# Three edits to the order of the first 450 microseconds of a transformer layer: gate columns stored as rows, later squares, earlier context products

## The chip, the cores and the metric

The kernel runs on one core of a Trainium2 chip. The metric is the device time of one execution in microseconds, the median of the runs. Engines are called as in the profile: PE (TensorE), DVE (VectorE), ACT (ScalarE), POOL (GpSimd), SP (SyncE, which here only issues transfers).

## What is computed

One layer over 1024 latent tokens and 256 context tokens of width 1024, in float32. Cut to what matters here:

```python
mod_lat = silu(c) @ w_ada + b_ada            # 6 x 1024 columns: sh1, sc1, gt1, sh2, sc2, gt2
mod_ctx = silu(c_ctx) @ w_ada + b_ada
h_lat = rmsnorm(x, g) * (1 + sc1) + sh1      # 1024 tokens
h_ctx = rmsnorm(ctx, g) * (1 + csc1) + csh1  # 256 tokens
rq, rk, rv, rg, nq, nk, nv, gates = split(h_lat @ w_in)
_, crk, crv, _, _, cnk, cnv, _ = split(h_ctx @ w_in)
...                                          # retention, neighbourhood attention over latent + context keys
x1 = x + gt1 * rmsnorm(merged @ w_o, g_post)
out = x1 + gt2 * rmsnorm(mlp(modulate(x1)), g_post_ffn)
```

The gates gt1 and gt2 (times the norm weights) are wanted late, as rows that multiply every token.

## The kernel before, in words

The kernel is written in program order, and a planner, which simulates the engines when the program is built, lays down the order of the instructions of each engine; each engine, and each transfer queue, then runs its own list in order. Where several instructions are ready in the simulation, the one that is earlier in the program goes first. `behind(ins)` forces the instructions of a block behind `ins` on its engine's list. Tiles come from pools of few buffers; a tile waits until the last reader of the buffer's former tile is done, and where one pool is closed and another opened on the same place, the new pool's tiles wait for the old pool's readers, transfers included.

Products are made in three passes of split float32 (`mm3`, lines 200 to 202): high x high, high x low and low x high, where `split` (lines 166, 167) casts the high part on ACT and subtracts the low part on DVE or POOL. Products of 512 (or 256) columns and eight blocks of the inner dimension are 24 instructions of PE. Their results lie in five PSUM banks taken in turn (`acc`), and ACT or DVE copies them out.

*Start.* The eight token tiles of x are loaded; `normed` (line 292) takes the squares' sums of four tiles on ACT (line 296), the reciprocal root on DVE (lines 214 to 225) and scales the tiles (line 299). `ada_first(p)` (line 323) makes the columns of shift and scale for a quarter of the width, with sixteen small products per weight block (line 332), and writes them to s1 and b1 (lines 338 to 341). `modulated` (line 311) turns a block of four tiles with PE (line 315), and writes the modulated block of hT (or of hc for the context): the high part by ACT (line 316), the full value hh by DVE (line 318), the low part by DVE or POOL (line 319). Line 345 normalises the first four tiles, line 349 the other four, and the loop from line 350 runs over the four quarters of the width.

*First projections.* `first` and `second` are the two weight chunks of the neighbourhood attention's keys, in two buffers of high and low parts. `fm_lat` makes their latent products (copied out at line 385, stored to k_na at line 392), `fm_ctx` their context products (copied to stc at line 398, stored to ck_na at line 399). The order in lines 434 to 437 is latent of first, latent of second, context of first, context of second. The weights of the values (`values`, line 488) are the next to be cast into these buffers (winhi by ACT at line 166, winlo by DVE at line 167). In between in the program stands the decay block (lines 440 to 465): z is loaded by SP, DVE makes zt (lines 443 to 454) with one exponential by ACT (line 445).

*Gate columns.* The rest of the modulation (`ada_rest`, line 405) is made in eight pieces, one beside each projection; the last one (n == 11) reads all of them back as columns (`columns`, line 272), multiplies the two gates by the norm weights (line 431), and POOL stores the columns [128, 8] to the rows `grow` in memory (line 432). They are read again at lines 955 and 1197. Then the pool `pb` is closed, and the neighbourhood stage opens its pool there; its keys kk are cast by ACT at line 623 and DVE at line 624, and enter PE's scores at line 648, among gate products (line 704) that fill PE.

Of the kernel before, what the change touches and what calls it, by code (L numbers as in the profile page):

```python
# [11 lines left out]
F32 = mybir.dt.float32  # L12
F32R = mybir.dt.float32r
AF = mybir.ActivationFunctionType
# [76 lines left out]
def block_kernel(ctx: ExitStack, tc: tile.TileContext, x, c, ctx_in, c_ctx, w_ada, b_ada, n_pre_mix, n_post_mix,  # L91
                 n_pre_ffn, n_post_ffn, w_in, decay_logit, w_ret_out, rpb, w_na_out, w_o, w_ff1, w_ff2, tab, out):
    nc = tc.nc
    v, a, g, pe, sy = nc.vector, nc.scalar, nc.gpsimd, nc.tensor, nc.sync
# [21 lines left out]
    def behind(ins):  # L116
        return nullcontext() if ins is None else tc.issue_after(ins.ins)
# [17 lines left out]
    def psum(tag):  # L135
        return ps.tile([128, 512], F32, name=tag, tag=tag, bufs=banks[tag])
# [5 lines left out]
    ident = const.tile([128, 128], F32, name="ident")  # L142
# [7 lines left out]
    def scratch(name, n, shape):  # L150
        return [dram.tile(shape, F32, name=f"{name}{k}") for k in range(n)]
# [10 lines left out]
    grow = scratch("grow", 2, [1, D])  # L162
# [79 lines left out]
    s1 = const.tile([128, 8, 2], F32, name="s1")  # L242
    b1 = const.tile([128, 8, 2], F32, name="b1")
# [17 lines left out]
    with ExitStack() as st:  # L261
        hT = [big.tile([128, 2, 8, 512], F32R, name="hT", tag=f"big{k}") for k in range(2)]
# [3 lines left out]
        def load_in(c0, **kw):  # L266
            return wp.load(w_in[0, :, c0:c0 + 256], 8, 256, **kw)
# [24 lines left out]
        def normed(tiles):  # L292
            n = len(tiles)
            ss = pa.tile([128, n], F32, name="ss", tag=f"ss{n}", bufs=2)
            for t, xt in enumerate(tiles):
                a.activation(hc[:, 1, 4:8, :].rearrange("p k n -> p (k n)"), xt[:], AF.Square, accum_out=ss[:, t:t + 1])
            r = rstd_of(pa, ss[:], n, f"x{n}")
            for t, xt in enumerate(tiles):
                v.tensor_scalar(xt[:], xt[:], r[:, t:t + 1], None, ALU.mult)

        xs, cxs, loads = [], [], []
# [9 lines left out]
        def modulated(xs, f, hi, lo, m, lo_eng):  # L311
            w = len(xs) * 128
            pt = psum("pt")
            for t, xt in enumerate(xs):
                pe.transpose(pt[:, t * 128:(t + 1) * 128], xt[:, f * 128:(f + 1) * 128], ident[:])
            a.activation(hi, pt[:, :w], AF.Identity, bias=b1[:, f, m:m + 1], scale=s1[:, f, m:m + 1])
            hh = pa.tile([128, 512], F32, name="hh", tag="hh", bufs=2)
            v.tensor_scalar(hh[:, :w], pt[:, :w], s1[:, f, m:m + 1], b1[:, f, m:m + 1], ALU.mult, ALU.add)
            lo_eng.tensor_tensor(lo, hh[:, :w], hi.bitcast(F32), op=ALU.subtract)

        pcol = psum("po")[:, 0:32].rearrange("p (b m) -> p b m", m=2)

# [23 lines left out]
        ada_first(0)  # L346
        first = load_in(2560, lo_eng=g, parts=4)
        loaded(x, 4, 8, xs)
        normed(xs[4:])
        for p in range(4):  # L350
            if p < 3:
                loads.append(ada_first(p + 1))
            if p == 1:
                second = load_in(2560 + 256, lo_eng=g)
            if p == 2:
                loaded(ctx_in, 0, 2, cxs, loads[2])
                normed(cxs)
            for half in range(2):
                for f in (2 * p, 2 * p + 1):
                    modulated(xs[half * 4:half * 4 + 4], f, hT[half][:, 0, f, :], hT[half][:, 1, f, :], 0, (v, g)[half])  # L360
            for f in {3: range(8)}.get(p, ()):
                modulated(cxs, f, hc[:, 0, f, :], hc[:, 1, f, :], 1, v)

# [13 lines left out]
        def fm_lat(w, ch, dst, p_, scale=1.0, silu=False, blocks=False):  # L377
            for f in range(2):
                stg = row()
                for half in range(2):  # L380
                    p = feature_major(w, lambda t, k: t[:, k, f * 128:(f + 1) * 128], half)
                    so = stg[:, half * 512:(half + 1) * 512]
                    if blocks:
                        so = stg[:].rearrange("p (b r c) -> p r b c", r=16, b=8)[:, half * 8:(half + 1) * 8]
                        a.activation(so, p[:].rearrange("p (r b c) -> p r b c", r=8, b=8), AF.Copy, scale=scale)
                    elif silu:
                        sgm = prb.tile([128, 512], F32, name="sgm", tag="kw", bufs=2)
                        a.activation(sgm[:], p[:], AF.Sigmoid)
                        v.tensor_tensor(so, p[:], sgm[:], op=ALU.mult)
                    else:  # L390
                        a.activation(so, p[:], AF.Copy, scale=scale)
                sy.dma_start(dst[ch * 2 + f][:], stg[:])

        def fm_ctx(w, r0, p_):
            for f in range(2):
                p = feature_major(w, lambda t, k: t[:, k, f * 128:(f + 1) * 128], 0, True)
                stc = p_.tile([128, NCTX], F32, name="stc", tag="stc", bufs=2)
                a.copy(stc[:], p[:])
                sy.dma_start(ck_na[r0 + f * 128:r0 + (f + 1) * 128, :], stc[:])
# [3 lines left out]
        pb = pool(st, "pb", 1)  # L403

        def ada_rest(n):
            ev = pb.tile([128, 512], F32, name="ev", tag="ev", bufs=1)
            for kb in range(2):
                w = wp.raw(4, 512)
                sy.dma_start(w[:], w_ada[0, kb * 512:(kb + 1) * 512, n * 512:(n + 1) * 512].rearrange("(k p) n -> p k n", p=128))
                for k in range(4):  # L410
                    s_ = cs[:, kb * 4 + k, 0:1]
                    if kb + k == 0:
                        v.tensor_scalar(ev[:], w[:, k, :], s_, None, ALU.mult)
                    else:
                        v.scalar_tensor_tensor(ev[:], w[:, k, :], s_, ev[:], ALU.mult, ALU.add)  # L415
            es = prb.tile([128, 2, 512], F32R, name="es", tag="kw", bufs=2)
            split(es[:, 0], es[:, 1], ev[:], lo_eng=g)
            pc = psum("po")[0:1, :]
            pe.matmul(pc, oner[:], es[:, 0], start=True, stop=False)
            pe.matmul(pc, oner[:], es[:, 1], start=False, stop=True)  # L420
            er = pb.tile([128, 512], F32, name="er", tag="ev", bufs=1)[0:1]
            a.copy(er, pc)
            sy.dma_start(arow[0:1, (n - 4) * 512:(n - 3) * 512], er)
            if n == 11:
                acol = pb.tile([128, 32], F32, name="acol")
                columns(pb, (arow[0],), acol[:])
                v.tensor_tensor(acol[:], acol[:], vt[:, 32:64], op=ALU.add)
                v.tensor_copy(b2[:], acol[:, 8:16])
                v.scalar_tensor_tensor(s2[:], acol[:, 16:24], 1.0, vt[:, 72:80], ALU.add, ALU.mult)
                for k, o in ((0, 0), (1, 24)):  # L430
                    v.tensor_tensor(acol[:, o:o + 8], acol[:, o:o + 8], vt[:, 80 + 8 * k:88 + 8 * k], op=ALU.mult)
                    g.dma_start(grow[k][0].rearrange("(k p) -> p k", p=128), acol[:, o:o + 8])

        fm_lat(first, 0, k_na, pb, blocks=True)
        fm_lat(second, 1, k_na, pb, blocks=True)
        fm_ctx(first, 0, pb)
        fm_ctx(second, 256, pb)


# [140 lines left out]
    with ExitStack() as sm:  # L580
# [6 lines left out]
        with ExitStack() as sn:  # L587
# [6 lines left out]
            for hp in range(4):  # L594
# [34 lines left out]
                for cb in range(8):  # L629
# [9 lines left out]
                    for e, (h, tbs, qs, ks) in enumerate(heads):  # L639
# [5 lines left out]
                        o = 0  # L645
# [32 lines left out]
                    for t in range(nb + 2):  # L678
                        for e in range(2):
# [6 lines left out]
                            last = pe.matmul(po[e * 64:(e + 1) * 64, o_:o_ + 128], l, r, start=(t == 0), stop=(t == nb + 1))  # L686
# [8 lines left out]
            for f, halves in [(f, (0, 1)) for f in range(NGB)] + [(f, (h,)) for h in range(2) for f in range(NGB, 16)]:  # L695
                w = wg.load(w_in[0, :, 3584 + f * 128:3584 + (f + 1) * 128], 8, 128, lo_eng=g)
                for half in halves:
                    hs = slice(half * 512, (half + 1) * 512)
                    stg = pn.tile([128, 512], F32, name="stg", tag="stg", bufs=3)
                    p = psum("mm")  # L700
# [147 lines left out]
        last = ret_finish(pna, *outs[3], lambda ob, hs: split(yr_[0][:, 3, hs], yr_[1][:, 3, hs], ob[:, hs]))  # L848


        for f in range(8):
            w = wn.load(w_na_out[0, :, f * 128:(f + 1) * 128], 4, 128, lo_eng=g)
            for half in range(2):
                hs = slice(half * 512, (half + 1) * 512)
                p = psum("mm")
# [12 lines left out]
    with sy_:  # L868
        pg = pool(sy_, "pg", 1)
        for f in range(8):  # L870
            w = wp.load(w_ret_out[0, :, f * 128:(f + 1) * 128], 4, 128, lo_eng=g)
            for half in range(2):
# [8 lines left out]
                p = acc()  # L881
                mm3(p[:], 4, lambda s_, k: w[s_][:, k, :], lambda s_, k: yr_[s_][:, k, hs])
                m = pg.tile([128, 512], F32, name="m", tag="m", bufs=2)
# [56 lines left out]
    with ExitStack() as s:  # L940
# [57 lines left out]
        xs = [php.tile([128, 2, D], F32, name="xn", tag="hp", bufs=2) for _ in range(2)]  # L998
# [21 lines left out]
        xs = [php.tile([128, 2, D], F32, name="xn", tag="hp", bufs=2) for _ in range(2)]  # L1020
# [53 lines left out]
        for j in range(EARLY):  # L1074
# [5 lines left out]
            with behind(turns[0] if j == EARLY - 1 else None):  # L1080
                p = product(acc(), ga, i + 1, b_1[:, 1])
# [4 lines left out]
        with behind(chain[-1]):  # L1086
            sums(raws[0])
            q3, last = third_sum(1)
# [101 lines left out]
    with ExitStack() as s:  # L1190
# [48 lines left out]
        for c4 in range(3):  # L1239
            w, new = home, None  # L1240
            for i, m in enumerate((m1, m2, m6, m3, m5, m7, m4)):
# [14 lines left out]
                for t in range(4):  # L1256
                    p = psum(next(turn8))
# [21 lines left out]
        for blkn in range(6, 8):  # L1279
# [15 lines left out]
            for t in range(8):  # L1295
# [8 lines left out]
                for cc in range(2):  # L1304
                    hs = slice(cc * 512, (cc + 1) * 512)
                    p = psum(next(turn8))
# [45 lines left out]
```

## Time and profile before

| | |
|---|---|
| runs | 1702.09, 1702.6, 1705.19 us; median 1702.6 |
| the profiled execution's own time | 1697.8 us |
| its span, first to last instruction | 1695.9 us |
| busy: PE, DVE, ACT, POOL | 96%, 58%, 38%, 20% of the span |
| mean granted clock of PE | 0.984 of full speed |

The span is what lies between the first and the last instruction of the trace; all times of instructions count from its start. The granted clock is the share of full speed that PE was given; 1.00 is 2.4 GHz and 0.50 is 1.2 GHz.

### The profile page before, as it was taken

To read this page: it belongs to the slowest core of one execution; us is meant where nothing else is said; L and a number is where in the kernel's file an instruction comes from. 1 tells how busy PE (TensorE), PEld (TensorE's weight loads), DVE (VectorE), ACT (ScalarE), POOL (GpSimd) and SP (SyncE) were. 2 spreads that over 40 slices of the span, in tenths; PEclk is the share of its full clock that TensorE was granted. 3 is DMA by queue.
4 is the path that set the end of the run, shared out by engine and by line. 5 is a ranking of instruction groups with operands and counts; after the bars stand their busy time and mean duration, and the time that the engine had idled before them with its cause. 6 is when DMAs were issued, how large, how long until landed. Compare 5 with 4: busy or idle time off the path is not lost. (4 is left out here: it accounts for less than half of the span.)

```text
span 1695.9 us, 21997 instructions
## 1 busy us (share of the span) xinstructions
PE 1622.1 (96%) x8547; PEld 1321.3 (78%) x8547; DVE 982.2 (58%) x1724; ACT 651.6 (38%) x912; POOL 338.9 (20%) x321
## 2 busy tenths in 40 slices
PE   5989999999999999989999998889999999999997
PEld 3889889988777777767776786668888878888885
DVE  5550244244345554565648657867776474778838
ACT  4321211112455555555346356334433365333311
POOL 1330022041322313357437001000010000000012
PEclk8999999999999999999999999999999999999998
DMA  9472644446523331276467424543354364423504
GB/s 326 163 172 71 185 137 150 145 131 190 148 72 121 98 101 62 87 207 179 137 229 250 163 84 142 176 166 112 138 179 168 132 253 149 173 101 111 183 30 149
DMA packets 156391, 252.95 MB, mean 149 GB/s; under 512 B 9776, under 2 KB 98872, under 8 KB 152576
## 3 DMA queue, kind: packets, MB, share of 16 engines
q1 hardware_dynamic: 145472, 213.05, 39.4%
q0 software_dynamic: 10816, 38.50, 6.4%
q8 instruction: 67, 1.10, 0.3%
q14 instruction: 36, 0.29, 0.1%
HBM read 184.18 MB, written 68.90 MB: 149 GB/s over the span
## 5 line engine op out<-in xcount | busy, mean ns | idle before, releaser
L166 ACT CAST wfhi<-wfraw 128x2048 fp32r<-128x2048 f32 (+2 forms) x47 | 62.0, 1357 | 175.7 <-PE sloc L201 36.9
L200 PE MATMUL mm<-hT,wghi 128*128 128x512 f32 x256 | 103.4, 404 | 0.0
L201 PE MATMUL mm<-hT,wghi 128*128 128x512 f32 x256 | 101.3, 396 | 0.0
L202 PE MATMUL mm<-hT,wglo 128*128 128x512 f32 x256 | 101.0, 395 | 0.0
L166 ACT CAST ops<-hr 128x2048 fp32r<-128x2048 f32 x20 | 38.2, 1909 | 113.2 <-PE mm L201 42.7
L167 DVE TENSOR_TENSOR wflo<-wfraw,wfhi 128x2048 fp32r<-128x2048 f32 (+2 forms) x47 | 74.2, 1605 | 5.8 <-ACT wfhi L166 5.8
L167 DVE TENSOR_TENSOR winlo<-winraw,winhi 128x2048 fp32r<-128x2048 f32 (+1 forms) x16 | 30.8, 1948 | 76.4 <-ACT winhi L166 76.4
L167 POOL TENSOR_TENSOR wglo<-wgraw,wghi 128x1024 fp32r<-128x1024 f32 x20 | 48.2, 2408 | 134.6 <-ACT wghi L166 134.5
L1312 POOL TENSOR_TENSOR m<-m,g 128x512 f32<-128x512 f32 x12 | 15.3, 1294 | 292.6 <-ACT jk L1311 292.6
L167 DVE TENSOR_TENSOR ops<-hr,ops 128x2048 fp32r<-128x2048 f32 x20 | 45.8, 2290 | 32.0 <-ACT ops L166 32.0
L166 ACT CAST winhi<-winraw 128x2048 fp32r<-128x2048 f32 (+2 forms) x21 | 27.4, 1335 | 95.5 <-PE sctx L201 48.8
L200 PEld LDWEIGHTS mm<-hT,wghi 128*128 128x128 f32 x256 | 48.4, 189 | 10.0 <-issue 2.2
L202 PEld LDWEIGHTS mm<-hT,wglo 128*128 128x128 f32 x256 | 48.5, 190 | 9.1 <-issue 0.3
L201 PEld LDWEIGHTS mm<-hT,wghi 128*128 128x128 f32 x256 | 48.4, 189 | 7.7 <-issue 0.2
L202 PE MATMUL sloc<-hT,winlo 128*128 128x512 f32 x136 | 53.3, 392 | 0.0
L200 PE MATMUL sloc<-hT,winhi 128*128 128x512 f32 x136 | 53.2, 392 | 0.0
L201 PE MATMUL sloc<-hT,winhi 128*128 128x512 f32 x136 | 53.1, 390 | 0.0
L201 PE MATMUL mm<-hT,winhi 128*128 128x512 f32 x120 | 47.4, 395 | 0.0
L415 DVE SCALAR_TENSOR_TENSOR ev<-winraw,cs,ev 128x512 f32<-128x512 f32 x56 | 44.6, 797 | 3.9 <-DMA winraw<-in_w_ada_dram 2.2
L202 PE MATMUL mm<-hT,winlo 128*128 128x512 f32 x120 | 46.8, 390 | 0.0
L607 POOL TENSOR_TENSOR tb<-tt,mask 128x128 f32<-128x128 f32 x56 | 29.4, 553 | 86.4 <-DVE mc L655 47.0
L200 PE MATMUL mm<-hT,winhi 128*128 128x512 f32 x120 | 46.4, 393 | 0.0
(1205 smaller groups left out, 5119.7 us busy)
## 6 DMA issues: line engine op xcount, KB each, us to landing
winraw<-in_w_ada_dram SPq DMA_DIRECT2D x24, 1024.0 KB
wfraw<-in_w_ff_dram SPq DMA_DIRECT2D x20, 1024.0 KB
winraw<-in_w_in_dram SPq DMA_DIRECT2D x14, 1024.0 KB
hs_d<-hs POOLq DMA_DIRECT2D x12, 1024.0 KB, 5.1
hr<-hs_d SPq DMA_DIRECT2D x12, 1024.0 KB
wgraw<-in_w_in_dram SPq DMA_DIRECT2D x20, 512.0 KB
gates<-stg POOLq DMA_DIRECT2D x32, 256.0 KB, 3.8
gg<-gates SPq DMA_DIRECT2D x32, 256.0 KB
```

The lines of the kernel that those rows point to most:

```text
L166: first = (hi_eng or a.copy)(hi_out, src)
L167: (lo_eng or v).tensor_tensor(lo_out, src, hi_out.bitcast(F32), op=ALU.subtract)
L200: pe.matmul(ps, lh, rh, start=(k == 0), stop=False)
L201: pe.matmul(ps, lh, rl, start=False, stop=False)
L202: pe.matmul(ps, ll, rh, start=False, stop=(k == ks - 1))
L415: v.scalar_tensor_tensor(ev[:], w[:, k, :], s_, ev[:], ALU.mult, ALU.add)
L607: g.tensor_tensor(tb[:, b * 128:(b + 1) * 128].rearrange("p (r c) -> p r c", c=8), tv[:, b0 + b], mask[:, c0 + b * 128:c0 + (b + 1) * 128] ...
L1312: (v if t >= 6 else g).tensor_tensor(y[cc], y[cc], g2[:, hs], op=ALU.mult)
```

## The change

There are three edits. `modulated` returns its ACT instruction, and the squares of the second four tiles are traced after the first half's two modulated blocks of the first quarter, with `behind`, in place of before the loop. The two finished gate columns, with the rest of their tile, are turned by one PE transpose into a PSUM bank, copied by DVE to a tile of rows and stored by POOL, eight rows of 128 floats for each gate, in place of the store of columns. And `fm_ctx(first)` is traced before `fm_lat(second)`.

```diff
-            a.activation(hi, pt[:, :w], AF.Identity, bias=b1[:, f, m:m + 1], scale=s1[:, f, m:m + 1])
+            first = a.activation(hi, pt[:, :w], AF.Identity, bias=b1[:, f, m:m + 1], scale=s1[:, f, m:m + 1])
...
             lo_eng.tensor_tensor(lo, hh[:, :w], hi.bitcast(F32), op=ALU.subtract)
+            return first
...
         loaded(x, 4, 8, xs)
-        normed(xs[4:])
         for p in range(4):
...
             for half in range(2):
                 for f in (2 * p, 2 * p + 1):
-                    modulated(xs[half * 4:half * 4 + 4], f, hT[half][:, 0, f, :], hT[half][:, 1, f, :], 0, (v, g)[half])
+                    last = modulated(xs[half * 4:half * 4 + 4], f, hT[half][:, 0, f, :], hT[half][:, 1, f, :], 0, (v, g)[half])
+                if p + half == 0:
+                    with behind(last):
+                        normed(xs[4:])
...
                 for k, o in ((0, 0), (1, 24)):
                     v.tensor_tensor(acol[:, o:o + 8], acol[:, o:o + 8], vt[:, 80 + 8 * k:88 + 8 * k], op=ALU.mult)
-                    g.dma_start(grow[k][0].rearrange("(k p) -> p k", p=128), acol[:, o:o + 8])
+
+                pt0 = psum("pt")
+                pe.transpose(pt0[:32, :128], acol[:], ident[:])
+                rows = pb.tile([32, 128], F32, name="rows", tag="rows32", bufs=1)
+                v.tensor_copy(rows[:], pt0[:32, :128])
+                for k, o in ((0, 0), (1, 24)):
+                    g.dma_start(grow[k][0].rearrange("(k p) -> k p", p=128), rows[o:o + 8, :])
 
         fm_lat(first, 0, k_na, pb, blocks=True)
+        fm_ctx(first, 0, pb)
         fm_lat(second, 1, k_na, pb, blocks=True)
-        fm_ctx(first, 0, pb)
         fm_ctx(second, 256, pb)
```

## Rows read from the trace of the kernel before

**Rows 1.** page of the profile, part 1: busy time of each engine.
```profile
PE 1622.1 (96%) x8547; PEld 1321.3 (78%) x8547; DVE 982.2 (58%) x1724; ACT 651.6 (38%) x912; POOL 338.9 (20%) x321
```

**Rows 2.** waits of PE, whole span: what it waited for: us in total, times, longest.
```profile
PE sctx L200 <- ACT hT L316: 4.3, 1, 4.3
PE sloc L648 <- DVE kk L624: 2.4, 1, 2.4
PE sloc L200 <- ACT winhi L166: 2.2, 1, 2.2
```

**Rows 3.** timeline of ACT: start us, us, line, operation, out<-in, count [idle before <-releaser].
```profile
19.77 2.18 ACT L166 CAST winhi<-winraw 128x512 fp32r<-128x512 f32 x4 [7.76 <-DMA winraw<-in_w_in_dram]
21.86 1.05 ACT L296 ACTIVATE hc<-xt 128x1024 fp32r<-128x1024 f32 x1
24.09 1.43 ACT L316 ACTIVATE hT<-pt,b,s 128x512 fp32r<-128x512 f32 x2
26.59 1.06 ACT L296 ACTIVATE hc<-xt 128x1024 fp32r<-128x1024 f32 x1
```

**Rows 4.** timeline of DVE, 20 to 33 us.
```profile
20.80 1.03 DVE L341 TENSOR_TENSOR s<-s,vt 128x2 f32<-128x2 f32 x2
30.15 2.74 DVE L299 TENSOR_SCALAR xt<-xt,r 128x1024 f32<-128x1024 f32 x4
```

**Rows 5.** timeline of PE, 29 to 35 us.
```profile
29.50 1.94 PE L332 MATMUL sloc<-winraw,cs 128*32 128x256 f32 x16
33.82 1.07 PE L332 MATMUL sloc<-winraw,cs 128*32 128x256 f32 x16
```

**Rows 6.** timeline of ACT, 92 to 106 us.
```profile
92.42 0.56 ACT L316 ACTIVATE hc<-pt,b,s 128x256 fp32r<-128x256 f32 x1 [0.56 <-PE pt L315]
102.95 0.21 ACT L445 ACTIVATE zt<-zt 128x16 f32<-128x16 f32 x1 [8.66 <-DVE zt L444]
103.33 1.90 ACT L166 CAST winhi<-winraw 128x2048 fp32r<-128x2048 f32 x1
```

**Rows 7.** timeline of SP's DMA queue, 88 to 96 us.
```profile
91.89 0.32 SPq L392 DMA_DIRECT2D k_na<-row  x1
92.31 2.25 SPq L441 DMA_DIRECT2D z<-in_ret_decay_logit_dram  x1
```

**Rows 8.** timeline of DVE, 93 to 109 us.
```profile
93.60 0.42 DVE L319 TENSOR_TENSOR hc<-hh,hc 128x256 fp32r<-128x256 f32 x1
102.53 0.18 DVE L443 TENSOR_SCALAR zt<-z 128x16 f32<-128x16 f32 x1 [8.51 <-DMA z<-in_ret_decay_logit_dram]
106.42 2.29 DVE L167 TENSOR_TENSOR winlo<-winraw,winhi 128x2048 fp32r<-128x2048 f32 x1
```

**Rows 9.** timeline of PE, at 108.77 us.
```profile
108.77 0.58 PE L201 MATMUL sloc<-winlo,hc 128*128 128x256 f32 x1 [2.06 <-DVE winlo L167]
```

**Rows 10.** busy by stretch: length; PE, PEld, DVE, ACT, POOL (instructions); granted clock, DMA share, GB/s.
```profile
27.06:29.50 2.44, 2.44 (x6) 1.50 (x6) 2.01 (x10) 0.68 (x2) 0.00 (x0) 0.50 1.09 349
108.77:113.70 4.93, 4.93 (x23) 4.93 (x24) 4.46 (x30) 0.58 (x2) 0.00 (x0) 0.50 0.83 254
448.24:451.40 3.16, 3.16 (x10) 2.68 (x11) 1.76 (x3) 2.21 (x4) 1.29 (x1) 0.50 0.44 123
```

**Rows 11.** timeline of DVE, 434 to 437 us.
```profile
434.59 0.19 DVE L283 COPY acol<-pt 128x32 f32<-128x32 f32 x1 [3.56 <-PE pt L282]
436.11 0.24 DVE L431 TENSOR_TENSOR acol<-acol,vt 128x8 f32<-128x8 f32 x2
```

**Rows 12.** timeline of POOL, then of ACT, 436 to 449 us.
```profile
436.78 1.80 POOL L432 DMA_DIRECT2D grow<-acol  x2
446.84 2.18 ACT L623 CAST kk<-kf 128x512 fp32r<-128x512 f32 x4 [10.88 <-DMA grow<-acol]
```

**Rows 13.** DMA issues: line's transfer, queue, count, KB each, median us from issue to landing.
```profile
grow<-acol POOLq DMA_DIRECT2D x2, 4.0 KB, 9.1
zp<-in_na_rpb_dram POOLq DMA_DIRECT2D x1, 14.5 KB, 2.1
```

## The prediction, made before the changed kernel was run

> **What bounds the kernel now.** I read the page's busy times first: PE is busy for 1622.1 of 1695.9 us [rows 1], so the kernel can get faster only where PE stands still or runs at the low clock, and every us of either that goes away is a us of the end, unless a new wait takes it. So the next view is what PE waited for, over the whole span [rows 2]; the reader is to see there three waits that touch lines of the change: 4.3 us for the first modulated block hT, 2.2 us for the weights winhi of the values, 2.4 us for kk, the first keys of the neighbourhood stage. The timelines around these three places say what held them, and the busy times by stretch say at which of its two clock levels PE came back: after each of them the granted clock was 0.50 (1.2 GHz) [rows 10].
>
> **First place, 20 to 33 us.** ACT is free of its weight casts at 21.95, the scale s1 is ready at 21.83 (20.80 + 1.03), but ACT then does two squares of the second half and turns to the first hT at 24.09 [rows 3, 4]. The change queues all four squares behind the two hT. ACT's work from 21.9 to 27.7 is the same in either order, so the squares still end at about 27.7 and DVE's scaling of the second half at 30.15 stays where it is. The first hT comes 24.09 - 21.95 = 2.1 us earlier, and with it PE's first product and DVE's remainder blocks behind it. The bounds are 0 and 2.1 us of gain. What PE can do with the time is little: six products, then the second block's sixteen column products (29.50), then transposes that need the scaled second half, then the next sixteen (33.82) [rows 5]. If the last ones move ahead of the transposes, as their weights come from a transfer and not from the squares, 1.07 us is won (their duration at full clock). I take 1.1. No DMA and no SP instruction moves with it. The cover of the second half's normalisation is ACT and DVE time in which PE has those products to do; gone, each us of delay of DVE's scaling at 30.15 is a us of PE. The added wait puts the squares behind the second hT on ACT; queued behind them is only the next hT, and DVE's square-root chain waits for them.
>
> **Second place, 92 to 114 us.** The four context products (24 products each) are the last PE work ahead of the values' weights. The weights of `first` sit in one of two buffers, and the values' first winhi takes that buffer, so it must wait until `fm_ctx(first)` has read it. Before, that is the third of four steps; with the change it is the second, with part of the second chunk's latent products and `fm_ctx(second)` still to come. The context blocks themselves are ready only at 94.02 (last remainder, 93.60 + 0.42) [rows 8], so the buffer can be free from about 94.5. But the buffer is not all that held the cast: ACT had nothing to do from 92.98 to 102.95, where it stood at the exponential of zt (L445), which waits for DVE, which waits for the transfer of z, issued at 92.31 and there at 102.53 [rows 6 to 8]. The cast follows at 103.33, its remainder winlo at 106.42, and PE's first product with winlo starts at 108.77 after another 2.06 us of idle [rows 6, 8, 9], and then runs 4.93 us at the low clock [rows 10].
> So the terms are: nothing, if cast and remainder stay behind the exponential; at the most both idle times, 2.2 + 2.06 (0.38 between them is small), and half of the low-clock stretch, 4.93 x 0.5 = 2.5, together 6.8; and below nothing, if the context copies (stc) are put behind the exponential on ACT: they hold PSUM banks until 103, and `fm_ctx(second)` cannot start; what it then does after 103 fills the stall that was there, so I price that at -0.5. Which of them it is depends on the order that the planner gives ACT and DVE. I expect the cast ahead of the exponential: it is ready at 94.5, while the transfer of z is only issued at 92.31 [rows 7]. DVE's first zt step stays ahead of winlo, and waits for z as now. Then winlo starts after z and three short steps, at 102.53 + 0.6 = 103.1 in place of 106.42 [rows 8]: 3.3 us. I take that and no gain of clock. Moved with the step are two stores of the context keys (SP), which come some us earlier, and the fourth store of k_na (91.89), which comes later, past z.
> That z is late is read in the rows: the 512 KB store of k_na went onto the same queue 0.4 us ahead of it, and z took 10.2 us [rows 7, 8]. The Trainium skill (DMA: Bandwidth & Descriptors, section "Queues, rings and completion order") says that each DMA engine takes turns between queue rows, packet by packet, and consumes one row's ring in order. By that rule z, with no store ahead of it in its own ring, would come earlier and the sum would take the third rival's value; no run here shows it.
>
> **Third place, 436 to 452 us.** The two gate columns are finished at 436.35 (436.11 + 0.24) and stored from [128, 8] element by element; the two stores are issued until 438.58 and land 9.1 us after issue, and ACT stands 10.88 us until 446.84 before kk, whose buffer lies where acol was [rows 11 to 13]. PE runs dry 2.4 us before 448.24 and then has 3.16 us at the low clock [rows 2, 10]: 2.4 + 1.6 = 4.0 us. The change adds one transpose on PE (0.24 us for the like one; as it also waits for its turn, up to the 3.56 us that DVE waited for the one before it [rows 11]), one copy on DVE (0.19, the row of the acol copy) and replaces the stores by two of eight runs of 512 B. Issue I leave at 1.80 for both [rows 12]. Landing lies between 2.1 us (the zp load, 8 partitions of long runs) and 9.1 (nothing gained) [rows 13]; it is nearest to zp, and I take 3. So the stores have landed at 436.35 + 0.5 + 0.2 + 1.8 + 3 = 441.9, with a late turn of the transpose at 445. PE needs kk's casts to begin by about 444.4 (448.24 - 2.4 - the 1.4 from the first cast to its product). I take the whole 4.0; the bounds are -0.8 (the transpose, the copy and a short wait of PE for the columns, no gain) and 4.0. DVE's copy stands in front of nothing before 440; behind the stores on POOL nothing waits but work that ACT's own stall holds. What is late next is PE itself.
>
> **Sum.** 1.1 + 3.3 + 4.0 = 8.4 us. The profiled execution took 1697.8 us (span 1695.9 and 1.9 around it), 4.8 below the median of the three runs, 1702.6. So 1689.4 against the profile, and 1694.2 against the median, which I forecast. 0.2% is 3.4 us, about what a measurement of this kernel can tell from no change.
>
> **The rivals.**
> *Only the columns count.* Cast and remainder stay behind the exponential, and the start's 2.1 us is spent in front of the transposes. For it: DVE's and ACT's stall on z is there whatever PE does [rows 6, 8]. Against it: the cast is ready before z. Gain 4.0: 1698.6. Chance 0.24, of which 0.15 is over 3.4.
> *Nothing is won.* The change does not do what it says: kk waits for another owner of its place, or each stall is filled by the next, as the order of every queue is planned anew. For it: three places of a few us each among 74 us of idle (1695.9 - 1622.1). Against it: the wait names grow [rows 12]. 1702.6. Chance 0.15.
> *z comes early too.* Without the store ahead of it, as above, both idle times and the low clock of the second place go: 1.1 + 6.8 + 4.0 = 11.9, 1690.7. Chance 0.14.
> *Slower.* The context products now stand ahead of the second chunk's, so PE reaches each of the eight context blocks soon after its transposes; from ACT's start to the end of DVE's remainder a block takes 94.02 - 92.42 = 1.6 us [rows 6, 8], and PE's queue is in order. Before, those products came after 91 us, when all but the last block were done. Full stalls would be 8 x 1.6 = 12.8, less the 5.1 of the other places: 7.7 slower, 1710.3; it decides from 0.65 us a block, and from 1.1 it is over 0.2%. Against it: the latent blocks are made the same way between 57 and 70 us, and PE has no wait for them. Chance 0.13.
>
> **How the numbers follow.** The forecast has 0.34. Faster: 0.34 + 0.14 + 0.15 = 0.63; within 0.2%: 0.09 + 0.15 = 0.24; slower: 0.13. The range reaches from below the early z, 1689.0, to just over no change, 1704.0, and leaves out the slower rival and the tails. Faster alone would be 1689.0 to 1699.2.
>
> **What would show it.** Right: on ACT the two hT before any square of the second half, PE's first product near 22.8; winhi of the values cast before zt's exponential and PE's wait for winlo near 2 us in all; grow landing in 2 to 4 us, ACT's idle before kk under 6 us, no wait of PE at L648, no 0.50 behind it. Wrong: the exponential still ahead of the cast with idle as before, a new wait of PE on hc in 70 to 95 us, or kk waiting for something other than grow.

## The result, and the profile after

The changed kernel took 1691.5 us (median of 4 runs, 1690.56 to 1695.82) against 1702.6 before: a ratio of 0.9932, 95% interval 0.9914 to 0.9949, so 11.1 us less. Run again later it gave 0.9947 (0.993 to 0.9963). The forecast was 1694.2. Its profiled execution took 1690.6 us (span 1688.8).

Lines have moved: 332 is now 333, from 361 to 431 each is three further (392 is 395), and from 432 on nine further (443 is 452, 623 is 632).

PE's waits over the whole span of the changed kernel (what it waited for: us in total, times, longest):

```profile
PE sctx L200 <- ACT hT L316: 2.4, 1, 2.4
...
PE po L337 <- DVE ev L335: 1.1, 2, 0.5
```

Of the three waits of [rows 2] those for winhi and kk are gone, and that for hT is shorter; a small one for DVE's copy ev, once 0.5 before, now comes twice. The busy times by stretch (length; PE, PEld, DVE, ACT, POOL; granted clock, DMA share, GB/s) say the same of the second and third places, and something else of the first:

```profile
30.00:34.00 4.00, 4.00 (x30) 2.38 (x33) 3.44 (x9) 0.00 (x0) 0.00 (x0) 0.50 1.09 348
34.00:36.00 2.00, 2.00 (x18) 0.73 (x18) 0.06 (x1) 0.00 (x0) 0.00 (x0) 0.50 1.10 348
...
40.00:120.00 80.00, 79.89 (x516) 69.20 (x515) 45.33 (x121) 30.05 (x47) 31.05 (x37) 1.00 0.60 185
420.00:460.00 40.00, 40.00 (x204) 32.85 (x203) 15.88 (x50) 19.66 (x36) 13.96 (x16) 1.00 0.50 154
```

PE idles 0.1 us in 40 to 120 us and not at all in 420 to 460, both at full clock: nothing of [rows 10] is left there. But from 30 to 36 us it is granted 0.50. The timelines of the changed kernel (start us, us, engine, line, operation, out<-in, count [idle before <-releaser]), PE at the start:

```profile
21.92 0.80 PE L200 MATMUL sctx<-hT,winhi 128*128 128x512 f32 x1 [2.41 <-ACT hT L316]
...
27.18 1.94 PE L333 MATMUL sloc<-winraw,cs 128*32 128x256 f32 x16 [0.19 <-DMA winraw<-in_w_ada_dram]
29.66 1.01 PE L337 MATMUL po<-small,ev 128*128 128x2 f32 x4 [0.55 <-DVE ev L335]
30.61 1.93 PE L333 MATMUL sloc<-winraw,cs 128*32 128x256 f32 x16
32.47 1.54 PE L315 MATMUL pt<-ident,xt 128*128 128x128 f32 x6
33.94 1.94 PE L333 MATMUL mm<-winraw,cs 128*32 128x256 f32 x16
```

Three column blocks of sixteen products take 1.93 to 1.94 each; before, the first did, the second took 1.07 [rows 5] and the third 1.05. The transposes now stand between the second and the third. DVE of the changed kernel, at all three places:

```profile
29.18 0.42 DVE L335 COPY ev<-sloc 128x256 f32<-128x256 f32 x1 [0.47 <-PE sloc L333]
...
30.71 0.23 DVE L339 TENSOR_TENSOR b<-po,vt 128x2 f32<-128x2 f32 x2 [0.45 <-PE po L337]
30.86 2.73 DVE L299 TENSOR_SCALAR xt<-xt,r 128x1024 f32<-128x1024 f32 x4
...
85.40 0.17 DVE L452 TENSOR_SCALAR zt<-z 128x16 f32<-128x16 f32 x1
...
92.36 2.29 DVE L167 TENSOR_TENSOR winlo<-winraw,winhi 128x2048 fp32r<-128x2048 f32 x1 [0.75 <-ACT winhi L166]
```

The scaling at 30.86 has a copy and a bias step ahead of it that wait for PE. zt finds z there; winlo, at 106.42 before [rows 8], is 14 us earlier. ACT and SP's transfer queue of the same kernel:

```profile
21.09 1.45 ACT L316 ACTIVATE hT<-pt,b,s 128x512 fp32r<-128x512 f32 x2
22.43 1.05 ACT L296 ACTIVATE hc<-xt 128x1024 fp32r<-128x1024 f32 x1
...
86.22 0.22 ACT L454 ACTIVATE zt<-zt 128x16 f32<-128x16 f32 x1
...
90.42 1.91 ACT L166 CAST winhi<-winraw 128x2048 fp32r<-128x2048 f32 x1
...
438.63 1.66 ACT L632 CAST kk<-kf 128x512 fp32r<-128x512 f32 x3 [1.03 <-DMA grow<-rows]
```

```profile
74.07 0.83 SPq L395 DMA_DIRECT2D k_na<-row  x2
75.00 0.72 SPq L450 DMA_DIRECT2D z<-in_ret_decay_logit_dram  x1
87.04 0.32 SPq L395 DMA_DIRECT2D k_na<-row  x1
```

The squares stand behind the two hT, as the edit says. The transfer of z stands behind the second of the four k_na stores in SP's list, at 75.00; before, it stood behind the fourth, at 92.31 [rows 7]. That is a move which no edit names: the planner made it. At the third place POOL issues the store of rows, in its timeline; and the view of that tile ends with the time from issue to landing (least, median, most):

```profile
436.40 1.05 POOL L441 DMA_DIRECT2D grow<-rows  x2 [4.50 <-DVE rows L439]
```

```profile
DMA to landing us min/median/max: 1.5/1.6/1.6
```

It lands in 1.6 us in place of 9.1 [rows 13], and ACT's idle before kk is 1.03 in place of 10.88 [rows 12].

### The profile page after: what moved, and what is told of

The parts are those of the page before. It is cut to its first block, busy times and chain, and to the rows that moved or that the text cites. A ratio compares the mean times of both kernels' runs of the same rounds, so it can differ in the third digit from the quotient of the medians.

```text
span 1688.8 us, 21995 instructions
## 1 busy us (share of the span) xinstructions
PE 1623.5 (96%) x8548; PEld 1320.7 (78%) x8548; DVE 980.4 (58%) x1725; ACT 652.4 (39%) x912; POOL 339.2 (20%) x321
## 5 line engine op out<-in xcount | busy, mean ns | idle before, releaser
L201 PE MATMUL mm<-hT,winhi 128*128 128x512 f32 x128 | 50.8, 397 | 0.1
L200 PE MATMUL mm<-hT,winhi 128*128 128x512 f32 x128 | 49.9, 392 | 0.0
L677 ACT COPY pl<-pt 128x384 f32<-128x384 f32 (+1 forms) x64 | 28.8, 450 | 43.8 <-PE pt L675 43.6
```

Of the source, the lines that this page charges most:

```text
L200: pe.matmul(ps, lh, rh, start=(k == 0), stop=False)
L201: pe.matmul(ps, lh, rl, start=False, stop=False)
L677: a.copy(pl[:, :nk], ptl[:, :nk])
```

## How the runs are compared

A gain of some us is hard to see in the total: 29 runs of the kernel before on one chip went from 1695.6 to 1709.5. So beside the ratio each profile is read at four marks, all counted from PE's first column product of the modulation (13.95 us into the span of the kernel before, 12.77 to 14.51 in the others, with the loads). The marks are the starts of PE's first main product, of the last context product of the keys (`fm_ctx`), of the last context product of the values, and of the last store of the neighbourhood stage (y_na).

| kernel | first | keys | values | y_na | ratio (95%) |
|---|---|---|---|---|---|
| before | 11.0 | 88.9 | 102.3 | 719.3 | |
| before, second profile | 11.0 | 88.9 | 102.3 | 719.1 | |
| squares alone | 8.8 | 90.9 | 104.0 | 723.5 | 1.0022 (1.0001, 1.0043) |
| rows alone | 11.0 | 88.9 | 101.1 | 714.2 | 0.997 (0.995, 0.9989) |
| context alone | 11.0 | 89.0 | 94.5 | 715.0 | 0.9975 (0.9958, 0.9992) |
| z early alone | 11.0 | 89.0 | 95.6 | 714.2 | 0.9955 (0.9938, 0.9972) |
| columns' own place | 11.0 | 89.1 | 102.3 | 721.9 | 1.0022 (1.0011, 1.0034) |
| rows and context | 11.0 | 89.0 | 94.5 | 709.2 | 0.9922 (0.9897, 0.9946) |
| the same again | 11.0 | 89.0 | 94.5 | 708.6 | 0.9936 (0.9919, 0.9954) |
| rows and context, z late | 11.0 | 89.0 | 94.5 | 708.7 | 0.9927 (0.991, 0.9944) |
| rows and z early | 11.0 | 88.9 | 95.4 | 708.1 | 0.994 (0.9922, 0.9957) |
| changed | 8.8 | 91.4 | 96.8 | 711.1 | 0.9932 (0.9914, 0.9949) |
| changed, again | 8.8 | 91.4 | 96.9 | 711.7 | 0.9947 (0.993, 0.9963) |
| changed, PE filled | 10.0 | 89.7 | 95.1 | 709.5 | 0.9954 (0.9934, 0.9973) |

The two profiles of before agree within 0.3 us at each mark, and so do kernels that differ only behind a mark, except rows alone at the values'. From the y_na store to the end of the span the profiles take 963 to 972 us with no order in it, so the marks, not the ends, carry the comparison of the parts. The ratio is an estimate over the runs of both kernels, not the quotient of two medians.

## Experiments: the parts alone

*The squares alone* (the first edit, the rest as before):

> The squares' edit alone, on the kernel before. Theory A, from the trace of the changed kernel (its work ahead of the values ended at 104.6 us against 103.1 before, although the first product came 3.0 us earlier): the edit itself costs 1 to 2 us, so 1.5 us slower than before, the first product about 2 us earlier and the column products and transposes up to 37 us at a granted clock of 0.50. Theory B, the forecast: 1.1 us faster than before.

Measured: 1706.4 against 1705.2, a ratio of 1.0022 (1.0001 to 1.0043). PE's first product is 2.1 us earlier, as forecast, and the last context product of the keys 2.0 later, that of the values 1.7. The edit costs.

*The rows alone* (the third edit):

> The gate columns' edit alone, on the kernel before. Theory A: 4.0 us faster than before, no wait of PE at the first scores and no 0.50 behind it, grow landing in about 1.6 us. Theory B: the wait is taken over by the next one (keys or queries still under way), under 2 us faster.

Measured: 0.997 (0.995 to 0.9989). No wait for kk is left, grow lands in 1.6 us, the waits for winhi and winlo stay at 1.8 and 1.7. From the values' mark to the y_na store it takes 613.1 us, where before took 617.0: 3.9 for this place.

*The context alone* (the second edit):

> The context products' edit alone, on the kernel before. Theory A: both stalls ahead of the values and the low clock behind them go, because z is loaded between two stores of k_na and is there before the exponential: 6.5 to 7.5 us faster than before. Theory B, the forecast: z stays late, only the cast moves ahead of the exponential, 3.3 us faster.

Measured: 0.9975 (0.9958 to 0.9992). The waits for winhi and winlo are gone, and the values' mark is 7.8 us earlier. At the y_na store only 4.3 of it are left. The view of the waits says where most of it went; PE's wait for kk grew from 2.4 to 4.2, and one for a weight's low part is new:

```profile
PE sloc L648 <- DVE kk L624: 4.2, 1, 4.2
...
PE mm L202 <- POOL wglo L167: 0.9, 1, 0.9
```

The landing of the grow stores in the same kernel (least, median, most):

```profile
DMA to landing us min/median/max: 10.8/11.2/11.6
```

The stores too were issued 6.3 us earlier than before (430.43, against 436.78 in [rows 12]), but they took 11.2 us to land in place of 9.1 [rows 13]. In the five profiles with this wait it grows with the landing: 2.0, 2.4, 2.8, 3.9 and 4.2 us of wait for 8.7, 9.1, 9.5, 10.6 and 11.2 (before's second and first profile, z early, squares, context). It does not go by how early PE is: with the squares alone PE is late and waits 3.9, with z early it is early and waits 2.8. Why the landing varies is not shown.

*Rows and context* (the change without its squares):

> The change without its squares' edit. Theory A: the squares cost time in the changed kernel too, so this one takes 1 to 2 us less than the changed kernel's 1691.5, about 1690. Theory B: the squares give 1.1 us, so about 1692.6.

Measured: 0.9922 (0.9897 to 0.9946), 1690.9 us. From context alone it wins 5.8 more at the y_na store, of which the wait for kk that is gone was 4.2.

## Experiments: why the second place gained

Two things had changed: z comes earlier, and the buffer of `first` is read earlier. Theory A: z held the stall. Theory B: the buffer did. First z alone is made early:

```diff
+        z = pb.tile([128, 16], F32, name="z")
+        sy.dma_start(z[:], bcast_rows(decay_logit, 16))
         fm_lat(first, 0, k_na, pb, blocks=True)
         fm_lat(second, 1, k_na, pb, blocks=True)
         fm_ctx(first, 0, pb)
```

> The kernel before, with the load of z traced ahead of the first key products and nothing else changed; fm_ctx(first) stays third. Theory A (the stall ahead of the values hung on z, which stood behind two stores in SP's list): z lands long before the exponential, both waits of PE for winhi and winlo go, and the kernel is as much faster as with the context products' edit alone, 4 to 7 us. Theory B (the weights' buffer, read by fm_ctx(first) until 97 us, holds the cast): a wait of about 2 us stays, under 3 us faster.

Measured: 0.9955 (0.9938 to 0.9972). z is issued at 19.71 us, the context products stand where they stood, and both waits are gone; the values' mark is 6.7 us earlier. So z early alone cures the stall. Then the opposite, rows and context with z forced behind the last k_na store:

```diff
+        stored = fm_lat(second, 1, k_na, pb, blocks=True)
...
-        sy.dma_start(z[:], bcast_rows(decay_logit, 16))
+        with behind(stored):
+            sy.dma_start(z[:], bcast_rows(decay_logit, 16))
```

> The change without its squares' edit, and z forced behind the last store of k_na in SP's list, as it stood before the change. Theory A (an early z is needed): the waits for winhi and winlo come back, 3 to 7 us slower than without the forcing (1690.9). Theory B (with the buffer free earlier the planner puts the cast ahead of the exponential anyway): no wait, within 1.5 us of 1690.9.

Measured: 0.9927 (0.991 to 0.9944); nothing came back. The timelines of this kernel, ACT, DVE and SP's queue:

```profile
89.21 1.91 ACT L166 CAST winhi<-winraw 128x2048 fp32r<-128x2048 f32 x1
...
106.31 0.22 ACT L453 ACTIVATE zt<-zt 128x16 f32<-128x16 f32 x1 [3.84 <-DVE zt L452]
```

```profile
91.15 2.29 DVE L167 TENSOR_TENSOR winlo<-winraw,winhi 128x2048 fp32r<-128x2048 f32 x1 [3.76 <-ACT winhi L166]
105.87 0.19 DVE L451 TENSOR_SCALAR zt<-z 128x16 f32<-128x16 f32 x1 [2.25 <-DMA z<-in_ret_decay_logit_dram]
```

```profile
98.96 2.15 SPq L449 DMA_DIRECT2D z<-in_ret_decay_logit_dram  x1
```

z is later than it ever was, and cast and remainder both go ahead of the steps that wait for it. Either condition alone takes the stall away; it needed both, z late and the buffer read late, so that the weights' cast and remainder were laid behind zt.

*Rows and z early* asks what the context order adds (the z edit above, with the rows' edit):

> The kernel before with the columns turned to rows and the load of z taken ahead of the stores in the transfer list; the context products stay where they stood, and so do the squares. If the late z was all that the moved context products cured, it gives the same as the change without the squares: the waits for winhi and winlo gone, no wait for kk, about 1691 us, a ratio near 0.993. If the order of the context products has a worth of its own (the first values' context product ended as early with z held late), it stays 2 us or more behind, about 1693 to 1694 us.

Measured: 0.994 (0.9922 to 0.9957), 1692.7 where rows and context gave 1691.3 beside it on the same chip. It is 0.9 us behind at the values' mark and level at the y_na store. The new wait for wglo is not in it. So a line that moves one small load gives nearly all that the moved products give; a difference of 1.3 us lies within the intervals.

## Experiments: why the third place gained

Is it the store's slowness, or only that kk lies where acol lay? The columns are put in a buffer that kk does not take, and stored element by element as before:

```diff
-                acol = pb.tile([128, 32], F32, name="acol")
+                acol = prb.tile([128, 32], F32, name="acol", tag="kw", bufs=2)
```

> The kernel before, its gate columns in a buffer that the keys kk do not take; still stored element by element, no transpose. Theory A (the long store mattered only as the owner of kk's place): grow still lands in about 9 to 11 us, PE does not wait at the first scores, and it is as much faster as the rows' edit alone, 4 to 6 us. Theory B (1024 elements of 4 bytes also hold up the loads of keys and queries): a wait of 1 us or more stays, under 3 us faster.

Measured: 1.0022 (1.0011 to 1.0034). The wait for kk is gone, yet PE waits 5.3 us a few products on. The timelines of this kernel, PE and ACT:

```profile
450.81 0.69 PE L648 MATMUL sloc<-kk,qh 128*128 128x384 f32 x1 [5.33 <-DVE mc L655]
```

```profile
439.06 0.62 ACT L623 CAST kk<-kf 128x512 fp32r<-128x512 f32 x1 [2.44 <-DMA kf<-k_na]
449.01 0.62 ACT L166 CAST qh<-qf 128x512 fp32r<-128x512 f32 x1 [9.33 <-DMA qf<-q_na]
```

ACT casts the keys early and then stands 9.33 us for a load of queries, DVE behind it 8.79 until its step on them (449.66), and PE behind DVE. The column stores, issued at 436.0 and 436.9, took 9.5 and 11.4 us to land, so until 445.5 and 448.3: the query load came in only after them. Taking away the shared place moves the wait from kk to qh; only the rows, landed in 1.6 us, take it away. The stretches of this kernel say the same of all transfers (columns as above):

```profile
436.00:438.00 2.00, 2.00 (x11) 1.65 (x10) 1.70 (x3) 0.62 (x2) 2.00 (x3) 1.00 0.92 292
439.00:447.00 8.00, 6.48 (x33) 5.14 (x31) 1.12 (x3) 0.62 (x1) 0.00 (x0) 1.00 0.64 48
449.00:451.00 2.00, 0.19 (x1) 0.19 (x2) 1.34 (x4) 1.99 (x3) 0.16 (x1) 0.90 1.00 196
```

While the element stores are under way the DMA engines are busy for 0.64 of the time and move 48 GB/s, against 292 and 196 on either side, with loads of keys and queries issued from 435.5 to 441.1. POOL's store of 256 KB of gates, issued among them at 437.76, took 11.5 us to land, where in the changed kernel such stores took 5.7 at most. So other transfers slow beside these stores; how they hold the loads back was not measured.

## Experiments: why the squares cost

The theory after the first runs: PE's earlier products leave it in the low clock longer. One kernel fills PE's wait for ev (0.55 at 29.66 in the changed kernel) with the second block's column products, made once more into an unused part of a bank; the spare results are read by nothing.

```diff
+                if p == 1 and j == 0:
+                    for kk in range(8):
+                        q = (kk % 4) * 32
+                        pe.matmul(spare[q:q + 32, 256:512], cs[:, kk, :], w[:, kk, :], start=(kk < 4), stop=(kk >= 4))
```

> The changed kernel, with the second block's eight column products of the first 30 us done a second time into a spare part of a bank (results not used), in the gap where PE waits for DVE's copy. Theory A (the squares' edit loses by the clock: PE starts earlier on work that comes at the pace of its loads, and the gaps keep it at 0.50): 1.00 is granted by about 34 us in place of 37, and the last context product ahead of the values is 1 to 2 us earlier than the changed kernel's 104.5. Theory B (it loses by the later scaling of the second half, 30.9 against 30.2 us): ahead of the values 104.5 or later.

Measured: 0.9954 (0.9934 to 0.9973), no faster in all than the changed kernel, but 1.7 us earlier at the keys' and values' marks, although the filler itself takes 1.04. PE of this kernel:

```profile
28.83 1.87 PE L334 MATMUL sloc<-winraw,cs 128*32 128x256 f32 x16
30.52 1.04 PE L340 MATMUL po<-winraw,cs 128*32 128x256 f32 x16
...
32.03 1.07 PE L334 MATMUL sloc<-winraw,cs 128*32 128x256 f32 x16
...
34.68 1.07 PE L334 MATMUL mm<-winraw,cs 128*32 128x256 f32 x16
```

The second and third column blocks take 1.07: full clock from about 30.5 on. Without the squares' edit it is the same; PE of rows and context, again:

```profile
28.37 1.53 PE L332 MATMUL sloc<-winraw,cs 128*32 128x256 f32 x16
...
32.69 1.07 PE L332 MATMUL sloc<-winraw,cs 128*32 128x256 f32 x16
33.58 1.05 PE L332 MATMUL mm<-winraw,cs 128*32 128x256 f32 x16
```

So what the edit costs goes with the clock of these blocks. It does not go with DVE's later scaling: counted from the first column product that starts at 17.8 in the filled kernel and at 17.7 in the changed one, and yet the filled kernel is 1.7 us ahead at the values' mark and only 0.6 behind rows and context, where the scaling starts at 16.3. But the filled kernel came to full clock before its filler had run, its first product was 1.2 us later than in the changed one, and the gap of 0.19 before the first block is missing in it. So the filler is not shown to be what brought the clock back, and that the gaps of PE (0.19 and 0.55) keep it low is not shown either.

## Experiments: the ends side by side

The changed kernel and rows and context, timed again on one chip, and a second profile of the kernel before:

> The changed kernel once more, beside the three that follow. If the squares' edit costs about 2 us, as the start of the kernel shows, it ends 1 to 3 us behind the next kernel, which lacks that edit: about 1692 against 1690 us where the kernel before gives 1703. If the edit gains what the prediction took (1.1 us), it ends about 1 us ahead of it.

> The change without its first part: squares, then the modulated rows, as before. Theory: the squares' edit brings PE's first product 3 us earlier and loses 5 us again on the way to the last context product, so this kernel is faster than the changed one by 1 to 3 us. Rival: the edit's 1.1 us are there in the sum and only this trace's start hid them; then it is slower by about 1 us. Between them, within 1 us, the runs don't tell.

> A second profile of the kernel before, with nothing changed. The profiled execution of before was one of its quicker ones (1697.8 us against a median of 1702.6). If the waits read in it are what the kernel always has, this profile shows the same ones: first hT near 24 to 25 us, a wait of about 2 us each for winhi and winlo, and 2 to 5 us for kk with a landing of grow of 9 us or more. If they are chance, one of them is missing here. The end of the run's stages should also tell where the other 4 to 5 us of a usual execution lie.

Measured: changed 1693.4 (1692.48 to 1695.65), without the squares 1691.3 (1690.2 to 1695.65), before 1702.2; ratios 0.9947 (0.993 to 0.9963) and 0.9936 (0.9919 to 0.9954). Four of the six runs without the squares lie below all six with them, and one more below all but one. With the marks, 2.3 to 2.4 us at the values' and 1.9 to 3.1 at y_na between two profiles of each, this says that the change is better without its first edit by about 2 us. The total alone would not prove it: the intervals overlap.

The second profile of before (1701.9 us) has the same waits, 1.9 for winhi, 1.6 for winlo, 2.0 for kk, and grow landing in 8.7 us. So both profiles have them.

## Why the prediction held, step by step

**What bounds the kernel: right.** PE's busy time hardly moved (1623.5, after 1622.1 [rows 1]); the gain lies in waits and low clock, and at the y_na store the profiles show 8.2 us of it (first profiles) and 7.4 (second). The forecast sum was 8.4; the medians gave 11.1 and 8.8, with intervals that overlap from 8.7 to 11.9. But the terms were not the forecast ones. That the sum came near is in part luck: at the values' mark the first term was 3.5 us too high and the second 4.5 too low.

**First place, +1.1: wrong, about -2.4 at the values' mark.** The first hT came 2.2 us earlier, as worked out. Two steps failed. The first is "DVE's scaling of the second half at 30.15 stays where it is". Counted from the first column product it went from 16.2 to 17.7. The planner put the copy of the first column block and a bias step into DVE's list ahead of the scaling; their waits for PE and their own time (0.47, 0.34 to the next start, 0.45, 0.15) are 1.4 of the 1.5. The second, and by the filled kernel the dearer one, priced the moved block at 1.07, "their duration at full clock": it ran at 0.50, as did the third. The three blocks took 5.81 us against 1.94 + 1.07 + 1.05 = 4.06 before, 1.75 more. What keeps the clock low there stays open.

**Second place, +3.3: the size was off.** It gave 7.8 at the values' mark, above the upper bound of 6.8 (the 0.38 that the bound left out, and 0.7 not assigned), and about 5 at the y_na store (714.2 to 709.2 on top of the rows). About 1 us of the rest is idle time of PE between the values' mark and the grow stores (1.2, in rows alone 0.1), the wait for wglo most of it; the remainder is not assigned. The step that failed is "DVE's first zt step stays ahead of winlo, and waits for z as now". z moved up in SP's list, so the outcome is that of the rival *z comes early too*, whose 6.8 is near the 7.8 measured and the 6.7 of z early alone. The buffer came free sooner than the 94.5 that was taken: the last remainder block of the context ended at 85.94, not at 94.02, and winhi was cast at 90.42. The rival's reason was half right: z left the place behind the late k_na store, but by the planner's order of the list; no run shows the rule of the Trainium skill (DMA: Bandwidth & Descriptors, section "Queues, rings and completion order") at work here, since z was issued 17 us sooner. And the forecast's own reason, cast ahead of exponential with z late, is real as well: forced, it was worth as much, since winlo also went ahead of zt.

**Third place, +4.0: right alone, 5.8 behind the second.** The landing was 1.6 where I took 3, ACT's idle 1.03, no wait at the scores, full clock behind. Alone it measured 3.9. The term was priced from one landing, 9.1; in the kernel with the second place alone the landing was 11.2 and the wait 4.2. On top of z early the rows won 5.9 from the values' mark on, with a wait of only 2.8, so the landing does not explain the whole difference.

**The rivals.** *Only the columns count* and *nothing is won* are out by the context alone. *Slower*: PE has no wait for hc in 40 to 120 us, so the eight context blocks cost nothing. A loss did turn up, but at another place, in the squares.

**Left open.** Why the clock comes back at 36 to 38 us with the squares' edit and at 29 to 32 without. Why the landing of the element stores varies from kernel to kernel. What varies by some us behind the y_na store; one part is a wait of PE in the retention, 4.1 us in this view of rows and context, again, 2.8 in the changed kernel's repeat, 0.5 in its first profile, 0.6 and 0.5 in the two of before, and it was not chased:

```profile
PE po L818 <- DVE sd L807: 4.1, 1, 4.1
```

## What to carry to other kernels

When an edit moves work in a planned kernel, look at every small transfer near it: which list it stands in, behind what, and what waits for it; one early load of z was worth nearly as much as moving the context products. Store a column as a row if its buffer or the loads behind it are wanted soon. A wait that hangs on a slow transfer is as uncertain as the landing of that transfer: read it in more than one profile before you price it. Price work moved to just behind a stall at the clock that PE has there, not at its full-clock duration.

## What was not expected of the hardware

The store of [128, 8] columns, 4 KB for each gate, landed in 8.6 to 11.6 us over six profiles; as eight rows of 512 B it landed in 1.5 to 1.6 in eight.

The granted clock of a stretch can miss a low one. In the second profile of before the windows give 1.00 where the column block takes the 1.94 us of a low clock; PE's timeline, and its stretch:

```profile
29.71 1.94 PE L332 MATMUL sloc<-winraw,cs 128*32 128x256 f32 x16
...
34.02 1.07 PE L332 MATMUL sloc<-winraw,cs 128*32 128x256 f32 x16
```

```profile
28.00:30.00 2.00, 2.00 (x9) 1.06 (x11) 1.66 (x11) 0.00 (x0) 0.00 (x0) 1.00 1.09 348
```

The filled kernel is another case: 1.00 over its whole start, though its first block at 28.83 took 1.87. The length of a group of like products is the surer reading.
